# Loading x as 16 x 8 rows in place of 128, in a batched fp32 matrix product

## The chip, the cores and the metric

The kernel runs on one core of a Trainium2 chip. The metric is the device time of an execution in microseconds (us). Most executions of one kernel agree within 0.3%.

## The reference

```python
batch, dim_i, dim_j, dim_k = 32, 256, 512, 384
# x: [32, 256, 512] float32, y: [32, 512, 384] float32
np.einsum('bij,bjk->bik', x, y).astype(np.float32)
```

The kernel reads 16.8 MB of x and 25.2 MB of y, and writes 12.6 MB.

## The kernel before

Four batches of x (Q = 4) are loaded at a time, 2 MB. They make 128 rows of 16 KB, which lie one after another in HBM; partition p gets row p. TensorE transposes x against an identity into PSUM (in fp32), ScalarE and VectorE copy the columns out as fp16, y is rounded to fp16, and products of 64 rows by 384 columns are collected and stored. All loads and stores are issued by SyncE into one queue.

```python
PQ = P // Q          # 32 partitions for each batch
R = I // PQ          # 8 rows of i in each partition: 8 x 512 x 4 B = 16 KB

def load_x(q):
    x_of[q] = x_pool.tile([P, R, J], F32, name="x_sb")
    keep(nc.sync.dma_start(
        out=x_of[q],
        in_=x[q * Q : (q + 1) * Q].rearrange("g (p r) j -> (g p) r j", r=R)))

def transpose(q, half):
    # ...
    t_ps = tpsum_pool.tile([P, 2, H, Q * PQ], F32, name="t_ps")
    for f in range(2):
        for h in range(H):
            keep(nc.tensor.transpose(
                t_ps[:, f, h], x_sb[:, h * NE + e + f, t::NJ], identity))
    # ... copies of t_ps to xt_sb, on VectorE and ScalarE in turn
```

Of the kernel before, what the change touches and what calls it, by code (L numbers as in the profile page):

```python
# [1 line left out]

# [5 lines left out]


MM_DT = mybir.dt.float16  # L10
F32 = mybir.dt.float32
P = 128


Q = 4
G = 2

LAG = 4


@with_exitstack
def kernel(
    ctx: ExitStack,
    tc: tile.TileContext,
    x: bass.AP,
    y: bass.AP,
    out: bass.AP,
):
    nc = tc.nc

    B, I, J = x.shape
    _, _, K = y.shape


    M = P // G
    NE = I // M
    NJ = J // P



    PQ = P // Q
    R = I // PQ
    H = R // NE
    U = B // G

    const_pool = ctx.enter_context(tc.tile_pool(name="const", bufs=1))
    x_pool = ctx.enter_context(tc.tile_pool(name="x_pool", bufs=3))
    y_pool = ctx.enter_context(tc.tile_pool(name="y_pool", bufs=5))
    yr_pool = ctx.enter_context(tc.tile_pool(name="yr_pool", bufs=2))
    xt_pool = ctx.enter_context(tc.tile_pool(name="xt_pool", bufs=2))  # L50
    o_pool = ctx.enter_context(tc.tile_pool(name="o_pool", bufs=5))
    tpsum_pool = ctx.enter_context(tc.tile_pool(name="tpsum", bufs=4, space=bass.MemoryType.PSUM))
    opsum_pool = ctx.enter_context(tc.tile_pool(name="opsum", bufs=4, space=bass.MemoryType.PSUM))


    keep = tc.keep_in_program_order

    identity = const_pool.tile([P, P], F32)
    make_identity(nc, identity)

    x_of, y_of, yr_of, xt_of, ps_of, o_of = {}, {}, {}, {}, {}, {}

    def load_x(q):
        x_of[q] = x_pool.tile([P, R, J], F32, name="x_sb")
        keep(
            nc.sync.dma_start(
                out=x_of[q],
                in_=x[q * Q : (q + 1) * Q].rearrange("g (p r) j -> (g p) r j", r=R),
            )
        )  # L70

    def load(u):

        if u == 0:
            load_x(0)
        if (u + 1) * G % Q == 0 and u + 1 < U:
            load_x((u + 1) * G // Q)
        y_of[u] = y_pool.tile([P, G, NJ, K], F32, name="y_sb")
        for g in range(G):
            keep(  # L80
                nc.sync.dma_start(
                    out=y_of[u][:, g],
                    in_=y[u * G + g].rearrange("(q t) k -> q t k", q=P),
                )
            )

    def transpose(q, half):

        x_sb = x_of[q]
        if half == 0:  # L90
            xt_of[q] = xt_pool.tile([P, NJ, NE, Q * PQ, H], MM_DT, name="xt_sb")
        n = 0
        for t in range(half * NJ // 2, (half + 1) * NJ // 2):
            for e in range(0, NE, 2):
                t_ps = tpsum_pool.tile([P, 2, H, Q * PQ], F32, name="t_ps")
                for f in range(2):
                    for h in range(H):
                        keep(
                            nc.tensor.transpose(  # L99
                                t_ps[:, f, h], x_sb[:, h * NE + e + f, t::NJ], identity  # L100
                            )
                        )
                dst = xt_of[q][:, t, e : e + 2].rearrange("c f p h -> c f h p")
                if n % 2 == 0:
                    keep(nc.vector.tensor_copy(dst, t_ps))  # L105
                else:
                    keep(nc.scalar.copy(dst, t_ps))  # L107
                n += 1

    def round_y(u):  # L110
        y_sb = y_of.pop(u)
        yr_of[u] = yr_pool.tile([P, G, NJ, K], MM_DT, name="y_r")
        for g in range(G):
            for t in range(NJ):
                if t % 2 == 0:
                    keep(nc.scalar.copy(yr_of[u][:, g, t], y_sb[:, g, t]))  # L116
                else:
                    keep(nc.vector.tensor_copy(yr_of[u][:, g, t], y_sb[:, g, t]))  # L118

    def multiply(u):  # L120
        xt_sb, y_r = xt_of[u * G // Q], yr_of.pop(u)
        ps_of[u] = []
        for e in range(NE):
            o_ps = opsum_pool.tile([P, K], F32, name="o_ps")
            ps_of[u].append(o_ps)
            for t in range(NJ):
                for g in range(G):
                    a = (u * G + g) % Q
                    keep(
                        nc.tensor.matmul(  # L130
                            o_ps[g * M : (g + 1) * M],
                            xt_sb[:, t, e, a * PQ : (a + 1) * PQ].rearrange("c p h -> c (p h)"),
                            y_r[:, g, t],
                            start=(t == 0),
                            stop=(t == NJ - 1),
                        )
                    )

    def collect(u):
        o_of[u] = o_pool.tile([P, NE, K], F32, name="o_sb")  # L140
        for e in range(NE):
            if e % 2 == 0:
                keep(nc.scalar.copy(o_of[u][:, e], ps_of[u][e]))  # L143
            else:
                keep(nc.vector.tensor_copy(o_of[u][:, e], ps_of[u][e]))  # L145
        del ps_of[u]

    def store(u):
        keep(
            nc.sync.dma_start(  # L150
                out=out[u * G : (u + 1) * G].rearrange("g (m e) k -> (g m) e k", e=NE),
                in_=o_of.pop(u),
            )
        )


    ahead = LAG - 2
    for u in range(ahead):
        load(u)
    for s in range(U + 2):  # L160
        if s + ahead < U:
            load(s + ahead)
        if s == 0:
            transpose(0, 0)
            transpose(0, 1)
        if s >= 2:
            collect(s - 2)
        if 1 <= s <= U:
            multiply(s - 1)
        if s < U:  # L170
            round_y(s)
        for half in range(2):
            q = (s + 1 - half) * G // Q
            if (s + 1 - half) * G % Q == 0 and 0 < q < B // Q:
                transpose(q, half)
        if s >= 2:
            store(s - 2)


# [1 line left out]
_INS = ['x', 'y']  # L181
_OUTS = [((32, 256, 384), 'float32')]


# [23 lines left out]
```

## Time and profile before

| | before |
|---|---|
| time, median | 135.93 us |
| span of the profiled run | 134.3 us |
| bytes moved | 54.5 MB |
| busiest compute engine | PE, 66% |
| packets of x: 1024 of 16 KB | median 0.611 us |
| packets of y and out: 6144 of 6 KB | median 0.234 us |

The last two rows come from the single packet records of the trace, which the page sums up in its DMA lines. The prediction below shows those lines. The strip of bytes gives GB/s in 40 equal slices of the span, here of the kernel before:

```profile
GB/s 112 415 400 450 409 417 421 456 388 421 417 448 408 409 428 421 457 394 417 413 443 436 408 417 428 442 422 402 425 423 444 426 402 427 419 427 419 417 394 158
```

It is flat: whatever is being moved, x, y or out, about 420 GB/s flow.

### The profile page before, as it was taken

What the parts mean: (1) busy time and instruction counts of PE and PEld (TensorE: products, weight loads), DVE (VectorE), ACT (ScalarE), POOL (GpSimd) and SP (SyncE); (2) the same over time, 40 slices, a digit from 0 to 9 for tenths busy, and PEclk for the clock granted to TensorE, in tenths of its full rate; (3) what the DMA queues carried; (4) which work ended last, traced back from release to release, by engine and by line L of the source; (5) the groups of instructions that cost most, each with busy time, mean ns of one, the idle gap of its engine ahead of it and who ended that gap; (6) DMA issues with size and microseconds to landing.
All of it is one profiled execution on the core that took longest, in us unless ns stands there. A gap on an engine that the chain in (4) does not pass through costs nothing.

```text
span 134.3 us, 1968 instructions
## 1 busy us (share of the span) xinstructions
PE 88.5 (66%) x768; PEld 73.2 (55%) x768; DVE 56.2 (42%) x128; ACT 63.9 (48%) x129; POOL 0.7 (1%) x6
## 2 busy tenths in 40 slices
PE   0049494979299767786099771976439986597920
PEld 0049474768177666666078661864427665476810
DVE  0004717471743365711634318460363425628620
ACT  3004837662762476712744428560475336738610
POOL 2000000000000000000000000000000000000000
PEclk9999999999959999999968999999965899779997
DMA  5999999999999999999999999999999999999993
GB/s 112 415 400 450 409 417 421 456 388 421 417 448 408 409 428 421 457 394 417 413 443 436 408 417 428 442 422 402 425 423 444 426 402 427 419 427 419 417 394 158
DMA packets 8073, 54.65 MB, mean 407 GB/s; under 512 B 896, under 2 KB 896, under 8 KB 7040
## 3 DMA queue, kind: packets, MB, share of 16 engines
q1 hardware_dynamic: 8064, 54.53, 97.8%
q8 instruction: 6, 0.10, 0.3%
q14 instruction: 3, 0.02, 0.0%
HBM read 41.94 MB, written 12.58 MB: 406 GB/s over the span
## 4 chain that ended last, share of the span: by engine, by line
DMA 78%; PE 13%; ACT 4%; DVE 0%; issue 0%
DMA y_sb<-in_y_dram 40%; DMA x_sb<-in_x_dram 38%; PE o_ps L130 9%; PE t_ps L99 3%; ACT xt_sb L107 2%; ACT y_r L116 1%; ACT o_sb L143 1%; DVE o_sb L145 0%
## 5 line engine op out<-in xcount | busy, mean ns | idle before, releaser
L130 PE MATMUL o_ps<-y_r,xt_sb 128*64 128x384 f16 x512 | 52.4, 364 | 28.5 <-ACT o_sb L143 20.8
L130 PEld LDWEIGHTS <-xt_sb 128*64 128x64 f16 x512 | 39.1, 121 | 38.8 <-issue 22.4
L116 ACT CAST y_r<-y_sb 128x384 f16<-128x384 f32 x64 | 29.5, 514 | 38.7 <-DMA y_sb<-in_y_dram 38.6
L99 PE MATMUL t_ps<-identity,x_sb 128*128 128x128 f32 x256 | 36.9, 301 | 11.4 <-DMA x_sb<-in_x_dram 11.4
L99 PEld LDWEIGHTS t_ps<-identity,x_sb 128*128 128x128 f32 x256 | 34.1, 211 | 16.0 <-issue 16.0
L118 DVE CAST y_r<-y_sb 128x384 f16<-128x384 f32 x64 | 20.0, 356 | 46.7 <-DMA y_sb<-in_y_dram 46.7
L107 ACT CAST xt_sb<-t_ps 128x512 f16<-128x512 f32 x32 | 22.4, 731 | 23.6 <-PE t_ps L99 23.6
L105 DVE CAST xt_sb<-t_ps 128x512 f16<-128x512 f32 x32 | 22.6, 728 | 24.1 <-PE t_ps L99 23.8
L145 DVE COPY o_sb<-o_ps 128x384 f32<-128x384 f32 x32 | 16.3, 544 | 2.1 <-PE o_ps L130 2.1
L143 ACT COPY o_sb<-o_ps 128x384 f32<-128x384 f32 x32 | 13.9, 492 | 1.3 <-PE o_ps L130 1.3
L107 ACT ACT_TABLE_LOAD x1 | 1.3, 1283 | 0.7 <-PEq L192 0.7
masks.py:199 POOL TENSOR_SCALAR_AFFINE_SELECT identity<-identity 128x128 f32<-128x128 f32 x1 | 0.3, 294 | 0.1
masks.py:197 POOL MEMSET identity<- 128x128 f32 x1 | 0.2, 206 | 0.3 <-POOLq L192 0.3
L192 POOL MEMSET const-bfloat16-1.0<- 128x1 bf16 x1 | 0.1, 102 | 0.0
L192 POOL MEMSET const-uint8-127<- 128x1 uint8 x1 | 0.1, 102 | 0.0
L192 POOL MEMSET const-float32-0.0<- 128x1 f32 x1 | 0.1, 99 | 0.2 <-issue 0.2
L192 POOL MEMSET const-float32-1.0<- 128x1 f32 x1 | 0.1, 99 | 0.0
## 6 DMA issues: line engine op xcount, KB each, us to landing
y_sb<-in_y_dram SPq DMA_DIRECT2D x32, 768.0 KB, 17.9
x_sb<-in_x_dram SPq DMA_DIRECT2D x8, 2048.0 KB, 20.8
out_dram<-o_sb SPq DMA_DIRECT2D x16, 768.0 KB, 17.8
```

The costliest lines, as they stand in the source:

```text
L99: nc.tensor.transpose(t_ps[:, f, h], x_sb[:, h * NE + e + f, t::NJ], identity)
L105: keep(nc.vector.tensor_copy(dst, t_ps))
L107: keep(nc.scalar.copy(dst, t_ps))
L116: keep(nc.scalar.copy(yr_of[u][:, g, t], y_sb[:, g, t]))
L118: keep(nc.vector.tensor_copy(yr_of[u][:, g, t], y_sb[:, g, t]))
L130: nc.tensor.matmul(o_ps[g * M : (g + 1) * M], xt_sb[:, t, e, a * PQ : (a + 1) * PQ].rearrange("c p h -> c (p h)"), y_r[:, g, t], start=(t ...
L143: keep(nc.scalar.copy(o_of[u][:, e], ps_of[u][e]))
L145: keep(nc.vector.tensor_copy(o_of[u][:, e], ps_of[u][e]))
L192: nc = _bacc.Bacc("TRN2", target_bir_lowering=False, num_devices=1)
```

## The change

The intent: the 16 DMA engines should read neighbouring 16 KB rows at a time, in place of stretches further apart. The source of the load becomes 16 x 8 rows, the second index stepping by 16 rows, so partition 8w + v gets row 16v + w. The transposes would then give columns in that order, so each writes its 128 columns with a step of 16 and puts them back.

```diff
+W = 16
...
                 out=x_of[q],
-                in_=x[q * Q : (q + 1) * Q].rearrange("g (p r) j -> (g p) r j", r=R),
+                in_=x[q * Q : (q + 1) * Q]
+                .rearrange("g (p r) j -> (g p) (r j)", r=R)
+                .rearrange("(v w) s -> w v s", w=W),
...
-                                t_ps[:, f, h], x_sb[:, h * NE + e + f, t::NJ], identity
+                                t_ps[:, f, h].rearrange("c (v w) -> c w v", w=W), x_sb[:, h * NE + e + f, t::NJ], identity
```

## The prediction

In it, a unit is the time of one packet of x, 0.611 us before the change, and d, in units, is how far one engine's packets lag behind another's. That a load of x would take 15.3 units in place of 8 is my estimate: it assumes that packets of x slow one another and that a lag spares them some of it (what the text calls sharing, and collisions). No trace of the kernel before shows either.

> **What bounds the kernel now.** I read the page first, for the busy shares and the strip of 40 slices, then the windows by stage, then the chain that ended last, then the instructions of the transposes, and last the single packet and semaphore records of the trace. From the page of the kernel before:
>
> ```profile
> span 134.3 us, 1968 instructions
> PE 88.5 (66%) x768; PEld 73.2 (55%) x768; DVE 56.2 (42%) x128; ACT 63.9 (48%) x129; POOL 0.7 (1%) x6
> ...
> DMA  5999999999999999999999999999999999999993
> ...
> q1 hardware_dynamic: 8064, 54.53, 97.8%
> ...
> DMA 78%; PE 13%; ACT 4%; DVE 0%; issue 0%
> ...
> L99 PE MATMUL t_ps<-identity,x_sb 128*128 128x128 f32 x256 | 36.9, 301 | 11.4 <-DMA x_sb<-in_x_dram 11.4
> ...
> y_sb<-in_y_dram SPq DMA_DIRECT2D x32, 768.0 KB, 17.9
> x_sb<-in_x_dram SPq DMA_DIRECT2D x8, 2048.0 KB, 20.8
> out_dram<-o_sb SPq DMA_DIRECT2D x16, 768.0 KB, 17.8
> ```
>
> The reader is to see that no compute engine is above 66%, while the packets of the one queue fill 97.8% of 16 DMA engines' span and the strip of DMA is 9 in every slice but the first and the last. The chain agrees: 78% of it is waiting for loads. A load of x or y lands some 18 to 21 us after its issue, so a deep backlog stands in front of the DMA engines, and an issue that comes a little late costs nothing.
>
> The windows split this by stage (us of the window; busy of each engine; clock, DMA share, GB/s):
>
> ```profile
> 1.80:8.60 6.80, 0.00 (x0) 0.00 (x0) 0.00 (x0) 0.21 (x1) 0.00 (x0) 1.00 0.95 351
> 8.60:110.00 101.40, 73.64 (x634) 61.35 (x636) 45.84 (x104) 51.41 (x104) 0.00 (x0) 0.93 1.01 423
> 110.00:125.00 15.00, 11.44 (x100) 9.25 (x98) 8.42 (x21) 9.20 (x20) 0.00 (x0) 0.89 1.02 423
> 125.00:134.30 9.30, 3.40 (x42) 2.62 (x38) 1.92 (x4) 2.01 (x5) 0.00 (x0) 0.91 0.76 313
> ```
>
> From 8.6 to 125 us the rate is flat at 423 GB/s, 26.4 GB/s for each of 16 engines. Only the first 7 us are slower. The packet records say what those are: an x packet is one 16 KB row to one partition, and its median is 0.611 us (16,384 B / 0.611 us = 26.8 GB/s); the mean of the first load is 0.735 us, those of the other seven 0.611 to 0.622 us. A 6 KB packet of y or out has a median of 0.234 us (26.3 GB/s). So in the steady part each engine runs at one fixed rate whatever it moves. In the last 9 us compute and stores finish together.
>
> [...]
>
> **The change, part by part.** The built program has the same instructions in the same order on all engines; only patterns differ.
>
> (a) The source of the x loads. Bytes (8 x 2 MB) and packets (8 x 128 of 16 KB) stay. The source is now [16][8][4096]: [...]
>
> Cost: unit = one packet, 0.611 us. Without sharing, a load is 8 units of each engine, 4.89 us. [...] How large is d? The 16 completions of the first load lie within 0.62 us in the trace's semaphore events; of later ones 14 of 16 lie within about 0.6 us and two about 1 us behind. A third of 0.62 us is a typical difference of two engines (estimate): d = 0.2/0.611 = 0.34. So a load takes 15.3 units, 9.36 us, 4.47 us more. Eight loads: +35.8 us, all of it on the bound, as the DMA engines have only about 3 us of idle time in the span. y and out keep their patterns and their 0.234 us.
>
> (b) What neighbouring rows could gain. Steady packets are at their median already; the seven later x loads have 0.37 us per engine to give ((mean-0.611) x 8 summed over them) and the first has (0.735-0.611) x 8 = 0.99 us. At most -1.4 us, and only if row distance causes the slow start. I take -0.5.
>
> (c) The transposes. 256 of them, 36.9 us busy, so 0.144 us each, now write with a step of 16 floats (64 B). If the write doubled them: +36.9 us of PE, 88.5 to 125. Under a DMA bound of 131 us that is hidden nearly everywhere, and more so with DMA at 167 us. On the path that ends last there is one batch of 16 (2.15 us in the chain before the last products): up to +2 us. I take +0.5. Copies out of PSUM read the same bytes as before: 0.
>
> Sum: 135.95 + 35.8 - 0.5 + 0.5 = 171.8. I name 168, [...].
>
> **The rivals.**
> - Only the source's locality matters (the change's intent): the slow start goes, 135. For it: first packets of 0.73 to 2.0 us against 0.611. Against: [...] it ends after two packets.
> - [...]
> - [...]
> - Collisions spread: [...] That adds to 172, perhaps up to 188.
> - PE becomes the bound through the strided writes: it would need a transpose of over 0.3 us each (88.5 - 36.9 + 256 x 0.31 = 131). I give this little.
>
> **Range and chances.** [...] 0.77 for more than 150. Some 0.08 for a partial loss of 3 to 14 us. 0.13 for within 2%, of which half is the intended gain without effect. Over 2% faster needs 2.7 us where at most 1.4 are to be had: 0.02. The range 140 to 188 leaves out the null cases below and a runaway above.
>
> **What would show it.** Right: x packets near 1.2 us while y and out packets stay at 0.234 us; GB/s of slices falling to about half wherever x is moving; the DMA strip still 9 everywhere, [...]; the first transposes starting some 4 us later than 8.7 us; a larger share of x in the chain of waits; PE below 60%. Step (c) shows in the transposes' mean of 301 ns. Wrong: x packets at 0.611 us and the first load landing by 8.6 us or earlier [...]; x packets slow in the first loads alone [...]; or a DMA strip with gaps and PE at 9s (PE the bound).

## The result, and the profile after

| | before | after |
|---|---|---|
| time, median (4 runs each) | 135.93 us | 175.84 us |
| ratio, 95% interval | | 1.293 (1.288 to 1.298) |
| span of the profiled run | 134.3 us | 174.5 us |
| x packets, median / mean | 0.611 / 0.630 us | 1.259 / 1.182 us |
| x packets, all, per engine | 40.3 us | 75.6 us |
| y and out packets, median / mean | 0.234 / 0.236 us | 0.234 / 0.248 us |
| y and out packets, all, per engine | 90.6 us | 95.2 us |

A ratio is the mean time of one kernel's fast runs over that of the other's fast runs of the same rounds, so it is not quite the ratio of the medians. "Per engine" is the sum of all packet times divided by 16.

From the page of the changed kernel: span, busy time, the strips of DMA share and GB/s, the queue, the chain by engine, the transposes (busy us, mean ns) and the issues.

```profile
span 174.5 us, 1968 instructions
PE 100.2 (57%) x768; PEld 81.2 (47%) x768; DVE 56.2 (32%) x128; ACT 64.1 (37%) x129; POOL 0.7 (0%) x6
...
DMA  5999989998999989999899999999999998999994
GB/s 150 210 220 381 210 185 404 398 210 184 382 420 299 214 275 421 432 251 222 311 415 432 231 198 340 420 420 225 192 372 417 390 222 196 394 425 424 422 415 196
...
q1 hardware_dynamic: 8064, 54.53, 98.2%
...
DMA 85%; PE 5%; ACT 3%; SPq 2%; DVE 1%; issue 1%; DVEq 0%
...
L104 PE MATMUL t_ps<-identity,x_sb 128*128 128x128 f32 x256 | 44.4, 344 | 40.4 <-DMA x_sb<-in_x_dram 40.4
...
y_sb<-in_y_dram SPq DMA_DIRECT2D x32, 768.0 KB, 23.2
x_sb<-in_x_dram SPq DMA_DIRECT2D x8, 2048.0 KB, 30.9
```

The bytes in the queue are the same 54.53 MB, and the engines are "busy" for the same share of a longer span: 98.2% against 97.8%. So the busy share does not tell a slow packet from a fast one. The GB/s strip does: dips to about 200 alternate with stretches of about 420. There are eight dips, one for each load of x, two or three slices long each, and after the last of them the strip stays at its old level. The windows of the changed kernel give the same by stage (us of the window; busy time of each engine; clock, DMA share, GB/s): the first load of x, and the last 15 us before the tail, in which no x is left to load:

```profile
1.80:13.10 11.30, 0.00 (x0) 0.00 (x0) 0.00 (x0) 0.22 (x1) 0.00 (x0) 1.00 0.97 224
...
150.00:165.00 15.00, 11.02 (x96) 9.28 (x96) 8.08 (x20) 9.27 (x20) 0.00 (x0) 0.89 1.02 423
```

The first x load fills 11.3 us at 224 GB/s, where the kernel before took 6.8 us at 351. Without x the rate is 423 GB/s, exactly that of before. The DMA share is about 1 in both windows (0.97 and 1.02).

So the time went into the packets of x. Per engine, x takes 75.6 - 40.3 = 35.3 us more, and y and out 95.2 - 90.6 = 4.6 us more. The sum, 39.9 us, is the whole difference: 135.93 + 39.9 = 175.8. What remains is why a packet of x takes twice as long.

### The profile page after: what moved, and what is told of

Its sections match the earlier page's. It is cut to its first block, busy times and chain, and to the rows that moved or that the text cites. A ratio compares the mean times of both kernels' runs of the same rounds, so it can differ in the third digit from the quotient of the medians.

```text
span 174.5 us, 1968 instructions
## 1 busy us (share of the span) xinstructions
PE 100.2 (57%) x768; PEld 81.2 (47%) x768; DVE 56.2 (32%) x128; ACT 64.1 (37%) x129; POOL 0.7 (0%) x6
## 3 DMA queue, kind: packets, MB, share of 16 engines
q1 hardware_dynamic: 8064, 54.53, 98.2%
## 4 chain that ended last, share of the span: by engine, by line
DMA 85%; PE 5%; ACT 3%; SPq 2%; DVE 1%; issue 1%; DVEq 0%
DMA y_sb<-in_y_dram 50%; DMA x_sb<-in_x_dram 35%; PE o_ps L135 4%; ACT xt_sb L112 1%; ACT y_r L121 1%; SPq L86 1%; PE t_ps L104 1%; SPq L69 1%; ACT o_sb L148 1%; DVE o_sb L150 1%; DVE y_r L123 0%; SPq L155 0%; DVEq L150 0%
## 5 line engine op out<-in xcount | busy, mean ns | idle before, releaser
L135 PE MATMUL o_ps<-y_r,xt_sb 128*64 128x384 f16 x512 | 56.2, 382 | 27.8 <-ACT o_sb L148 18.9
L104 PE MATMUL t_ps<-identity,x_sb 128*128 128x128 f32 x256 | 44.4, 344 | 40.4 <-DMA x_sb<-in_x_dram 40.4
L104 PEld LDWEIGHTS t_ps<-identity,x_sb 128*128 128x128 f32 x256 | 40.7, 217 | 45.7 <-issue 45.7
L135 PEld LDWEIGHTS <-xt_sb 128*64 128x64 f16 x512 | 40.5, 127 | 41.1 <-issue 22.3
## 6 DMA issues: line engine op xcount, KB each, us to landing
y_sb<-in_y_dram SPq DMA_DIRECT2D x32, 768.0 KB, 23.2
```

What stands on the lines that cost most here:

```text
L104: nc.tensor.transpose(t_ps[:, f, h].rearrange("c (v w) -> c w v", w=W), x_sb[:, h * NE + e + f, t::NJ], identity)
L135: nc.tensor.matmul(o_ps[g * M : (g + 1) * M], xt_sb[:, t, e, a * PQ : (a + 1) * PQ].rearrange("c p h -> c (p h)"), y_r[:, g, t], start=(t ...
```

## The experiments

Four explanations were open.

- *Ports*: which partitions are written at the same time decides how long a packet of x takes, and the new source pattern changes that (the prediction's theory). It is an assumption: no record names the engine or the path of a packet.
- *Rows*: reading neighbouring rows with all engines at once is slow in HBM.
- *Columns*: the transposes' strided PSUM writes are slow.
- *Issue*: SyncE's first issue, a load of x, takes 0.67 us where it took 0.38.

A later one is *place*: packets to some partitions may be slow by themselves, whatever is written beside them.

"Wrong on purpose" below means that the rows or columns of x come out in another order; the work is the same in size and in its engines.

### The load alone, and the columns alone

Each run takes one half of the diff: `load_alone` has the changed load with `t_ps[:, f, h]` as before, `columns_alone` the load of before with the strided `t_ps`. Their outputs are wrong, which doesn't matter for the times.

```diff
# load_alone, against the changed kernel
-  t_ps[:, f, h].rearrange("c (v w) -> c w v", w=W), x_sb[...], identity
+  t_ps[:, f, h], x_sb[...], identity
# columns_alone, against the changed kernel
-  .rearrange("g (p r) j -> (g p) (r j)", r=R).rearrange("(v w) s -> w v s", w=W),
+  .rearrange("g (p r) j -> (g p) r j", r=R),
```

For `load_alone` the ports theory, like the rows theory, has nothing change against the changed kernel.

> The changed load alone, transposes writing contiguous columns as before (the result is wrong on purpose: the columns stay out of order). If [...] reading neighbouring rows is slow in HBM (rows theory), nothing changes against the changed kernel: 175 to 176 us, x packets with a median near 1.26 us. If the strided PSUM write is the cause (columns theory): 136 us.

> The load of before, transposes writing with a step of 16 columns as changed (wrong on purpose: the columns are put out of order). Ports and rows theory: 136 us, and the transposes' median stays at 284 to 285 ns. Columns theory: about 176 us. A small cost of the strided write in the tail would show as +0.3 to +2 us.

Measured: `load_alone` 175.99 us (ratio 1.292), x packets with a median of 1.249 us. `columns_alone` 136.12 us, ratio 0.9999 (0.9984 to 1.0015). The transposes of each, first of `load_alone`, then of `columns_alone`:

```profile
L104 PE MATMUL t_ps<-identity,x_sb 128*128 128x128 f32 x256 | 43.8, 340 | 40.2 <-DMA x_sb<-in_x_dram 40.2
```

```profile
L102 PE MATMUL t_ps<-identity,x_sb 128*128 128x128 f32 x256 | 36.4, 299 | 9.9 <-DMA x_sb<-in_x_dram 9.9
```

The columns theory falls. It also shows a trap: the mean of a transpose rose from 301 to 344 ns in the changed kernel, which looks like the strided write at work. But the contiguous writes of `load_alone` show 340, and the strided ones of `columns_alone` 299. The mean goes with the granted clock of TensorE (the share of its full clock rate that it was allowed), 0.83 in the two slow kernels and 0.92 to 0.93 in the two others. Minimum and median of the transposes, which the view of one line gives, are 272 and 284 ns before and 273 and 285 after.

### Neighbouring or distant rows, as 16 x 8 or as before

The changed load differs in two things at once: the order of the rows in HBM and the pattern, 16 x 8 rows in place of 128. Two sources (wrong, with rows that overlap) separate them.

```diff
# far_rows_dealt_in_8, against the kernel before: 16 x 8 rows, 128 KB and 12 KB apart
-  out=x_of[q],
-  in_=x[...].rearrange("g (p r) j -> (g p) r j", r=R),
+  out=x_of[q].rearrange("p (v r) j -> p v (r j)", v=1),
+  in_=bass.AP(tensor=x.tensor, offset=q * Q * I * J, ap=[[8 * R * J, 16], [3072, 8], [1, R * J]]),
# near_rows_plain, against the kernel before: 128 rows 4 KB apart
+  in_=bass.AP(tensor=x.tensor, offset=q * Q * I * J, ap=[[1024, P], [1, R * J]]),
```

> Source pattern of 16 x 8 rows as in the change, [...] (at 12 KB, overlapping, [...]; wrong on purpose). Transposes as before. Ports theory: 173 to 178 us with x packets near 1.2 us. Rows theory (neighbouring rows are slow): 136 us with x packets at 0.61 us.

> Source pattern of 128 rows of 16 KB at a step of 4 KB (overlapping; wrong on purpose), [...]. Ports theory: 135 to 136.5 us, x packets at 0.611 us. Rows theory: about 175 us. If neighbouring rows cure the slow start, the mean of the first load's packets falls from 0.735 to below 0.65 us and the time by up to 1 us.

Measured: `far_rows_dealt_in_8` 175.89 us (ratio 1.292), x packets with a median of 1.235 us; `near_rows_plain` 136.72 us (ratio 1.0036, 1.0018 to 1.0055), median 0.611 us. The GB/s strips, first of the far rows as 16 x 8, then of the near rows as 128:

```profile
GB/s 132 229 190 409 199 194 399 408 203 192 379 425 309 199 285 422 426 255 230 319 421 428 226 208 333 422 422 203 200 384 423 377 226 193 406 425 425 423 399 199
```

```profile
GB/s 170 447 382 473 389 417 442 432 390 417 335 435 420 425 419 431 460 389 427 410 453 425 407 423 423 446 412 418 423 425 444 409 417 425 423 425 425 417 355 104
```

The dips follow the 16 x 8 pattern, not the distance of the rows. The rows theory falls. (Rows that overlap also read fewer different bytes of HBM than the real ones, which these two runs do not separate; `two_halves` and `near_rows_own_port` below do without overlap and agree.) Neighbouring rows did help where the change hoped: the first 16 packets take 0.78 to 1.23 us in place of 0.73 to 2.0, and the mean of the first load falls from 0.735 to 0.673 us, 8 x 0.062 = 0.5 us per engine. The time did not fall, though; it rose by 0.4%. The packet sums of the two kernels are equal (131.4 us per engine), so the 0.5 us was given back, visibly in the second eighth of the y and out packets (mean 0.251 us against 0.237); why there, I did not settle.

### The plain order in two halves

If the partitions that are written at the same time matter, the kernel before may become as slow when its x loads are merely cut at partition 64, with rows and columns untouched.

```diff
+  rows = x[q * Q : (q + 1) * Q].rearrange("g (p r) j -> (g p) r j", r=R)
+  for s in range(2):
+      keep(nc.sync.dma_start(out=x_of[q][s * 64 : (s + 1) * 64],
+                             in_=rows[s * 64 : (s + 1) * 64]))
```

> The kernel before, with each x load as two transfers to partitions 0-63 and 64-127, rows in order, contiguous columns, right result. [...] Ports theory: [...] 172 to 178 us, x packets near 1.2 us. Any theory of row order, of strided columns or of the issue path: about 136 us.

Measured: 177.72 us, ratio 1.305, result right; x packets with a median of 1.262 us. Its GB/s strip has the same dips:

```profile
GB/s 149 209 206 390 197 194 394 407 179 205 375 418 309 183 268 423 423 264 223 288 420 432 227 207 331 422 423 220 196 369 425 382 223 195 395 422 423 425 409 176
```

This kernel shares with the changed one neither the row order, nor the strided columns, nor the source of 16 x 8 rows. Against the kernel before only the transfers of x differ, 16 to 64 partitions each in place of 8 to 128, and its packets of x are as slow as those of the changed kernel (1.262 us and 1.259 us).

### Eight engines

> The change with W = 8 in place of 16, right result: [...] Ports theory: [...] about 246 us (235 to 260), x packets again near 1.2 us. Eight engines without any sharing: 16 units, 9.8 us a load, +39 us: about 175 us, x packets 0.61 us.

```diff
-W = 16
+W = 8
```

Measured: 270.16 us, ratio 1.984, result right. The direction and the rejection of 175 hold, the number missed: 246 was expected, 235 to 260 at the widest. The DMA strip and the queue of this run:

```profile
DMA  7999896758855995489944996469964899847674
...
q1 hardware_dynamic: 8000, 54.53, 76.9%
```

The strip has lost most of its 9s, and the queue fills 76.9% of the engines' span: some engines have nothing to do for part of the time. The packets also fit eight engines at work on x. The queue of the kernels before and after holds 896 packets of 4 bytes, 16 for each of 56 transfers; this run holds 832, which is 8 fewer for each of the 8 loads of x. (That each of them stands for one engine is my reading.) The x packets took 1.338 us in the mean where 1.17 was expected (the prediction's 9.36 us over eight packets). If eight engines carry them, that is 1024 x 1.338 / 8 = 171 us for each, 21 us more than the 150 that 1.17 us would give, which accounts for most of the miss. The 6 KB packets, too, were slowed, to a mean of 0.313 us.

The single packets say more. In the first load 88 of 128 packets of x took 1.75 to 1.85 us, and of the 272 packets of y that started beside it (4.6 to 27.3 us) 234 took 0.65 to 0.74 us: about three times 0.611 and three times 0.234, where the expectation had near 1.2 us for x and did not speak of y. What slowed them so stays open.

### The issue path

The kernel before with a setting of the program, `nc.dge_precook`, turned off, which should make every issue on SyncE longer:

```diff
     nc = tc.nc
+    nc.dge_precook = False
```

> [...] Every issue on SyncE should take longer. If the issue path costs the time: well over 136 us. Ports theory: within 0.5 us of before, as the transfers are issued some 18 us before they land.

Measured: 136.45 us, ratio 1.0017 (1.0002 to 1.0033). The first issues on SyncE, before and then in this run (start us, us, what):

```profile
0.74 0.38 SPq L66 DMA_DIRECT2D x_sb<-in_x_dram  x1
1.17 0.89 SPq L81 DMA_DIRECT2D y_sb<-in_y_dram  x2
```

```profile
0.73 0.58 SPq L67 DMA_DIRECT2D x_sb<-in_x_dram  x1
1.37 1.23 SPq L82 DMA_DIRECT2D y_sb<-in_y_dram  x2
```

Each issue is longer by about 0.2 us. The others hardly cost anything, as a load or store of the kernel before lands 17.8 to 20.8 us (median) after its issue; the first can, as the first packet starts at 2.09 us in place of 1.78. The theory of the issue path falls.

### Small loads by themselves

What is left is *ports* against *place*. Five small loads ahead of the first real one separate the two. In D I wanted half the engines to start some three packets late, which by my estimate makes its packets faster than those of C. The rival in the expectation is *place*:

```diff
+        if q == 0:
+            def probe(first, n, row, w):   # n rows to partitions first..first+n-1, as w x n/w rows
+                keep(nc.sync.dma_start(
+                    out=x_of[q][first : first + n].rearrange("p (o r) j -> p o (r j)", o=1),
+                    in_=rows[row : row + n].rearrange("(v w) s -> w v s", w=w)))
+            probe(0, 32, 0, 8)      # A
+            probe(64, 32, 32, 8)    # B
+            probe(64, 64, 64, 8)    # C
+            probe(96, 16, 0, 4)     # ahead of D
+            probe(0, 64, 64, 8)     # D
```

> The kernel before with five small loads of x rows ahead of the first real load, into the same tile (which the real load then overwrites, so the result stays right). Each has a source of few long-strided runs, [...]. A: partitions 0-31, [...]. B: partitions 64-95, [...]. C: partitions 64-127, [...]. [...] D: as C on partitions 0-63, [...]. Ports theory: A and B packets near 0.611 us after the first of each engine, C near 1.17 us [...], D near 0.75 us [...]. Rival, [...] B near 1.2 us, and C and D both near 1.2 us. The whole kernel: 20 to 35 us longer than before.

Measured, from the packet records: 

| load | packets | median us | mean us | expected us |
|---|---|---|---|---|
| A, partitions 0-31 | 32 | 0.611 | 0.647 | 0.61 |
| B, partitions 64-95 | 32 | 0.611 | 0.620 | 0.61 (place theory: 1.2) |
| C, partitions 64-127 | 64 | 1.268 | 1.198 | 1.17 |
| D, partitions 0-63 | 64 | 1.133 | 1.059 | 0.75 |

The windows of A, B and C in this run (DMA share and GB/s stand last; a share of half is that of eight of the 16 engines):

```profile
2.60:5.10 2.50, 0.00 (x0) 0.00 (x0) 0.00 (x0) 0.00 (x0) 0.00 (x0) 1.00 0.52 210
5.40:7.90 2.50, 0.00 (x0) 0.00 (x0) 0.00 (x0) 0.00 (x0) 0.00 (x0) 1.00 0.46 197
9.70:19.10 9.40, 0.00 (x0) 0.00 (x0) 0.00 (x0) 0.00 (x0) 0.00 (x0) 1.00 0.51 112
```

In A and B about half of the 16 engines are busy and 197 to 210 GB/s flow, 25 to 26 GB/s for each of eight, and 28 of the 32 B packets take 0.611 us to the nanosecond. (That the loads but the fourth use 8 engines each fits the packets of 4 bytes, too: the five loads add 4 x 8 + 4 = 36 to the 896. Which eight, no record says.) C has the same busy share, and half the bytes flow. This decides between the two: on partitions 64-95 alone, packets are as fast as on 0-31, and on 64-127 together, at the same share of the engines, they take twice as long. Two packets of 16 KB in 1.268 us, the median of C, are 25.8 GB/s, nearly what one packet at a time gives (26.8). So the number fits two packets that go at the rate of one; that they do was estimated from it, not seen.

D missed its number: 0.75 us rested on the planned lag of three packets, an estimate that did not come true. The first packets of D took 1.15 to 1.23 us, a slow start like that of the kernel before, which may have shortened the lag; no record tells the engines apart. So D says nothing about a lag.

The whole kernel took 169.68 us, 33.7 more than before, within the 20 to 35 expected: some of the five loads wait for earlier ones, and the first real load is issued only at 34.22 us.

### Neighbouring rows, to every fourth partition

At last the change's intent without its side effect, with a right result: four loads of 32 neighbouring rows, each to every fourth partition. The run can show whether packets are slowed, not which engine writes what.

```diff
# against the changed kernel
-W = 16
+W = 4
...
+  rows = x[q * Q : (q + 1) * Q].rearrange("g (p r) j -> (g p) r j", r=R)
+  N = P // W
+  for b in range(W):
+      keep(nc.sync.dma_start(out=x_of[q][b::W], in_=rows[b * N : (b + 1) * N]))
...
-  t_ps[:, f, h].rearrange("c (v w) -> c w v", w=W), x_sb[...], identity
+  t_ps[:, f, h].rearrange("c (b i) -> c i b", b=W), x_sb[...], identity
```

> The change's intent [...], right result: each x load as four transfers of 32 neighbouring rows to every fourth partition (b, b+4, b+8, ...), and the transposes write the columns back in order. Ports theory: [...] x packets at 0.611 us, 135 to 137 us. If neighbouring rows help the slow start, the first load's mean falls from 0.735 us towards 0.65 us, at most 0.7 us of the time; four times as many issues for x may take that back. Rows theory or a cost of splitting: over 150 us.

Measured: 136.93 us, ratio 1.0054 (1.0035 to 1.0073), x packets with a median of 0.611 us. The dips are gone. With four times the x loads the landing times are shorter, 12.9 us for x where it was 20.8:

```profile
y_sb<-in_y_dram SPq DMA_DIRECT2D x32, 768.0 KB, 12.4
x_sb<-in_x_dram SPq DMA_DIRECT2D x32, 512.0 KB, 12.9
out_dram<-o_sb SPq DMA_DIRECT2D x16, 768.0 KB, 12.4
```

The first load's mean was 0.773 us, no better than 0.735. The 0.8 us that the kernel lost is at least in part at the start: the four issues of x take 2.46 us, so the first load of y is issued at 3.24 us in place of 1.17, and the GB/s strip begins with 150, 305, 379 where it was 112, 415, 400. So the intent, freed of its side effect, brings nothing here: the kernel before already moves its packets of x at a median of 0.611 us, the least time seen. No experiment pointed to a version that beats both kernels.

## Why the prediction was right

It named 168 us, 140 to 188, and 175.84 was measured. By its own steps:

- *What bounds the kernel*: confirmed. The 39.9 us by which packets grew, summed per engine, came out in full as time; nothing hid them, and no compute engine stepped in.
- *Step (a), the cause*: that packets of x slow one another was assumed, and no record names an engine or a path. That 16 engines work on a load fits the packets (896 of 4 bytes before and after, 16 for a transfer), and packets near 1.2 us, as estimated, came out in `far_rows_dealt_in_8` (1.235 us), `two_halves` (1.262), load C of `ports_alone` (1.268) and, slower than estimated, in `eight_engines` (mean 1.338).
- *Step (a), its size*: +35.8 us was reckoned for x, +35.3 measured. The factor of about 15.3/8 on the unit of 0.611 us and the count of eight loads held; a mean packet of 1.169 us was implied and 1.182 measured. So close an agreement is partly luck. How a lag shortens a load was my estimate, which no run tests, and the lag d = 0.34 itself rests on a reading that holds only for the first four loads of the trace before: there the first 14 of a load's 16 completions lie within 0.4 to 0.6 us, but within 1.1 to 1.8 us in the last four. By the prediction's own rule (a third of the spread) that would be d of 0.6 to 1 for these. In the changed kernel the mean packet does fall, from 1.22 us in the second and third load to 1.15 and 1.16 us in the last two.
- *"y and out keep their patterns and their 0.234 us"*: this term was mis-sized. Their median kept, but 403 of 6144 such packets took over 0.3 us where 7 had before, 342 of them while a packet of x was in flight, and the sum grew by 4.6 us per engine. The prediction had this under its rivals ("Collisions spread") and left it out of the sum.
- *From 171.8 down to 168*: the wrong way. The 3.8 us were an allowance of mine, which nothing bore out. 171.8 plus the 4.6 for y is 176.4.
- *Step (b), -0.5 us*: nothing was gained. The first packets took 0.64 to 0.81 us in the changed kernel, but 0.87 to 1.21 us in `load_alone`, which has the same load, so even that start is not certain, and the first load's packets have a mean of 1.19 us in both. `near_rows_plain` shows the 0.5 us in the packets and no gain in the time. One reading was off without consequence: the means of the later loads and the 0.37 us count six 16 KB packets of another queue (instruction); without them the means are 0.611 to 0.620 us and 0.21 us were to be had.
- *Step (c), +0.5 us*: nothing; `columns_alone` is at 0.9999. What the prediction said would show this step, the transposes' mean, was a poor witness: it rose to 340 ns and more in every kernel with a granted clock of 0.83 or less, whichever way the columns were written, and stayed at 298 in `ports_alone`, which is slow at a clock of 0.95.
- *The rivals*: the gain from locality alone, 135 us, did not come (175.84); the packets of x were not slow in the first loads alone (three quarters took over 1.15 us, 71% still in the last load); PE did not become the bound (57%).
- *The signs it named*: most came. Packets of x near 1.2 us, half the GB/s while x moves, a full DMA strip, PE below 60%, and first transposes at 13.2 us in place of 8.7. One did not: x was to take a larger share of the chain that ended last, and it fell from 37.7% to 35.1%, while y rose from 40.2% to 50.2%. All transfers are in one queue, so a load of y that stands behind a slow load of x lands later too (23.2 us after its issue in place of 17.9); that the chain books this wait under y is the likely reason, not a tested one.

## What to carry to other kernels

A DMA pattern has a second effect beside the order of its bytes. In these runs a 16 KB packet of x took 0.611 us when a load was 128 rows to 128 partitions, or four times 32 rows to every fourth partition, and about 1.26 us when it was 16 x 8 rows to 128 partitions, or twice 64 rows to 64 neighbouring partitions. Before changing an access pattern for locality, measure a packet of the new one, and look at GB/s rather than at the DMA engines' busy share, which stayed at 98% though only 224 GB/s flowed in the first load of x, where 423 flowed without x. And where the packets already take the least time seen (0.611 us here, median and minimum alike in most loads), a better order has next to nothing to win: two ways of reading neighbouring rows brought none (136.72 and 136.93 us, against 136.13 in the same rounds).

## What stays open

- Which engine writes which partitions, and what the slow packets of x wait for: no record shows it. Measured are the rates: at a DMA share of about half, 112 GB/s flowed in load C of `ports_alone` and about 200 in A and B; the first load of x ran at 224 GB/s in the changed kernel and 351 before.
- Strided PSUM writes of other kinds: fp32 transposes of 128 columns written with a step of 64 B cost nothing, 299 ns in the mean against 301, 0.121 us from start to start (median) in both, time ratio 0.9999. Products were not tried.
- The slow first packets of the first load: 0.73 to 2.0 us before, 0.78 to 1.23 with neighbouring rows, against 0.611 later. Not every first load has them (0.61 to 0.71 us in load A of `ports_alone`, at a DMA share of 0.52).
- Which sources take the longer issue on SyncE: 0.67 us against 0.38 for the first load, and 0.58 with `nc.dge_precook` turned off alone. Whether the third dimension by itself adds to it was not tried.
